# Row-projection order, an earlier key norm and four seven-product pairs in the last row unit of a two-layer decoder trunk

## Chip, cores and metric

The kernel runs on one core of one Trainium2 chip. The metric is the device time of one execution in microseconds (us), the median of three runs. A separate execution was profiled; every row below comes from it.

## The reference

Two layers, 256 tokens, model width 2048, all in float32. Each layer normalises the residual stream, multiplies it by one input projection `w_in` (2048 x 6160), runs two head groups side by side, multiplies their outputs by `w_o`, adds the residual, and does the same with a squared-ReLU MLP of width 8192.

```python
h = rms_norm(x, attn_norm)
g_q, g_k, g_v, g_gate, g_lr, s_q, s_k, s_v = split(h @ w_in)
o_gla = gated_linear_attention(g_q, g_k, g_v, log_sigmoid(g_lr @ w_gate_up + b_gate) / 16)
o_gla = rms_norm(o_gla, gla_out_norm) * silu(g_gate)
sq, sk = rms_norm(heads(s_q), sb_q_norm), rms_norm(heads(s_k), sb_k_norm)
o_sb = rms_norm(stick_breaking(sq, sk, s_v), sb_out_norm)
x = x + concat(o_gla, o_sb) @ w_o
x = x + square(relu(rms_norm(x, mlp_norm) @ w_up)) @ w_down
```

The stick-breaking group has 8 heads of 128; each head's queries and keys are normalised over those 128 elements before the scores.

## The kernel before

**Precision.** A float32 product is made of three matmuls: both operands are split into a high part (ScalarE, tile `whi` for weights, L868) and a low part (VectorE, tile `wlo`, L872: the value minus its high part), and high x high, high x low and low x high are added in PSUM (L967 to L969, 128 x 512 outputs).

**Units.** The large projections are cut into units of 1024 output columns. A unit works through eight pairs of contraction tiles (256 rows of weights each). A pair is done in one of three ways. A plain pair takes 8 products (two token halves x two column halves x two tiles), so 24 matmuls, in two steps. A fast pair uses a seven-product scheme for 2 x 2 blocks: 7 products, so 21 matmuls, in four steps of 2, 2, 2 and 1 products; VectorE first forms sums of weight blocks (tile `ts` and two overwritten quarters of `raw`, all L749) and then four low parts instead of two. An added pair is a plain pair whose low part is not made on VectorE: ScalarE writes the negated high part (`dlo`, L876) and a DMA issued by GpSimd adds the raw weights to it (L879).

**Order inside a unit.** It is a list of pair numbers written by hand; each time a pair number occurs, that pair's next step is issued. `STEPSI` with fast pairs `FASTI` serves the first row unit, `STEPSR` with `FASTR = (1, 3, 4, 5, 6)` the other three, `STEPS` with `FAST = (1, 3, 5, 6)` the MLP units. Pairs 2 and 7 are added pairs in all of these.

**Row units.** Ahead of each layer's attention four units of `w_in` are computed for the next layer in the order `ROWS = ("iv", "ik", "qk", "sq")`: values, keys of the stick-breaking heads, queries and keys of the linear attention, queries of the stick-breaking heads. Their results stay in SBUF as natural rows (`natural[kind, half]`), scaled by the row norm at L1106. For layer 0 the four units stand at 33.6 to 196.1 us of the profile, for layer 1 at 1066.2 to 1229.9 us. In `big_unit`, the first row unit of layer 1 also transposes the new residual (`turned`, L556) after its first and after its second step.

**Attention.** `attend` first opens a scratch region (`begin`, the list `opened["att"]`) whose memory belonged to the units until their last piece is done (`using["mlp"]`). Pieces made with `core` wait for that opening and are listed in `using["att"]`; pieces made with plain `add` do neither. `keys_queries(0)` names the keys first and then the queries of the first four heads; `turn_heads` calls `heads_norm`, which for each of two row blocks squares (ScalarE, L1348), sums per head (VectorE, L1351), then forms the reciprocal root (L459 to L468) and multiplies the rows by it (VectorE, L1330); then the heads are transposed (L1378) and copied with their scale (L1386) for the scores. Each square needs one of five `t2` buffers, held until its sum is made; at the opening in layer 0 two of the five are held by the constants and one by the small gains. Beside this, `narrow` runs the remaining projections of `w_in` on TensorE (L1243 to L1245) with the same high and low parts; the first of them, `va`, has 256 value columns and the 16 low-rank columns (128 x 272 outputs, weight parts 128 x 544).

**What sets the order.** A planner (`Plan`) simulates the engines with rough lengths. TensorE, SyncE and GpSimd issue most pieces in the order in which the program names them; VectorE and ScalarE take, of the pieces that are ready and find their buffers free, the one with the earliest due time; the attention's own TensorE pieces (`apart`) go ahead of the line when ready. The resulting order is fixed in the program. On the chip each engine runs its list strictly in that order and waits at semaphores.

Of the kernel before, what the change touches and what calls it, by code (L numbers as in the profile page):

```python
# [17 lines left out]
P = 128  # L18
# [5 lines left out]
FAST = (1, 3, 5, 6)  # L24
# [11 lines left out]
FIRSTR = 1  # L36
STEPSI = [0, 0, 1, 3, 1, 2, 2, 1, 1, 3, 4, 4, 5, 5, 5, 6, 5, 6, 6, 6, 7, 7]
FASTI = (1, 5, 6)
ADDEDI = ADDED
ROWS = ("iv", "ik", "qk", "sq")  # L40
BIG = ("up", "down") + ROWS
ACTS = 17
DEPTH = 2
# [182 lines left out]
def trunk_kernel(  # L226
# [556 lines left out]
    def unit_order(u):  # L783

        if u.kind == "o":
            return (STEPSO, STEPSP)[u.n2], (FASTO0, FASTO)[u.n2]
        if u.kind in ROWS[FIRSTR:]:
            return STEPSR, FASTR
        if u.kind == ROWS[0]:
            return STEPSI, FASTI  # L790
        return STEPS, FAST
# [359 lines left out]
    def big_unit(u, was, tail, after_tail):  # L1151
# [11 lines left out]
        for k, j in enumerate(order):  # L1163
# [21 lines left out]
            if k < 2 and was and was.kind == "o":  # L1185
                n = 2 * was.n2 + k
                for h2 in range(2):
                    done["up", 0, 2 * n + h2] = turned(
                        n, h2, ((5, 7), (1, 6))[k][h2], hm, "mlp", u.l, "sxh"
                    )  # L1190
            if 0 <= u.l < DEPTH - 1 and k < 2 and (u.at("down", 3, 1) or u.kind == "iv"):
                n = k + 2 * (u.kind == "iv")
                for h2 in range(2):
                    done["in", 0, 2 * n + h2] = turned(
                        n, h2, ((5, 7), (1, 6))[k][h2], hN, "attn", u.l + 1, "sxh"
                    )
# [118 lines left out]

    def inv_rms(ss, n, width, hold, *deps):

        box = {}

        def mean():  # L1320
            own = norm_tile("ny", hold, n), norm_tile("nt", hold, n)
            box["rr"], box["parts"] = inv_rms_parts(ss(), n, width, own)
            box["parts"][0]()

        a = core("DVE", 0.16, mean, *deps)
        b = core("ACT", 0.42, lambda: box["parts"][1](), a)
        return (lambda: box["rr"]), core("DVE", 0.72, lambda: box["parts"][2](), b)
# [8 lines left out]

    def heads_norm(rows, w, *deps):

# [21 lines left out]
        got[0].takes.append(slot_hold)  # L1360
        rr, ready = inv_rms(ss, len(rows) * nh, P, slot_hold, got)
        muls = [
# [146 lines left out]
    def normed(po, hold, o, *deps):  # L1509

        a = core("ACT", 0.6, lambda: nc.scalar.activation(o(), po(), AF.Copy), *deps)
        release(hold, a)
        return a, heads_norm([(o, a)], 512)

# [41 lines left out]
    def attend(l):  # L1556
# [78 lines left out]
        def turn_heads(key, nat, nat_hold, c, w, dst, h0, scale, deps, *more):  # L1635

            muls = heads_norm(rows(nat, c, w, deps), w, *more)
            for i in range(0, w // P, 2):
# [529 lines left out]
```

## Time and profile before

| | us |
|---|---|
| median of 3 runs (lowest, highest) | 2123.29 (2123.22, 2123.62) |
| the profiled execution | 2123.44 |
| its span, first to last instruction | 2121.7 |
| TensorE busy | 2110.9 (99%) |
| VectorE busy | 1969.7 (93%) |
| ScalarE busy | 1600.7 (75%) |
| GpSimd busy | 175.7 (8%) |

The span is 1.7 us shorter than the execution's time. The records of matmuls overlap: a 128 x 512 matmul is shown with 0.39 us, but the next one starts about 0.227 us later, and a 128 x 272 one starts about 0.12 us after the one before. So a gap on TensorE is read from the distance of two starts, less that pace; the profile's idle figure counts only what is left after the modelled end. The granted TensorE clock is 1.00 of 2.4 GHz throughout.

### The profile page before, as it was taken

Reading aid. Unit: us, or ns where it says so; the run is one execution under the profiler, and the core shown is the slowest. Engines: PE = TensorE matmul, PEld = TensorE weight load, DVE = VectorE, ACT = ScalarE, POOL = GpSimd, SP = SyncE. Lnnn points to the kernel's source line nnn. Section 1 sums busy time; section 2 is a strip of 40 time slices with the busy share of each in tenths; the row PEclk is TensorE's granted clock in tenths of the full one; section 3 lists DMA queues with packets and bytes.
Section 4 is the critical chain, followed back from the end, with each engine's and each line's share of the span. In section 5 each row is a group of like instructions: output and inputs, shape, how many; then the busy total and the mean of one; then the engine's idle time right before and its main releaser. Section 6 shows DMA issues by size and latency. Waiting matters only on the chain.

```text
span 2121.7 us, 28669 instructions
## 1 busy us (share of the span) xinstructions
PE 2110.9 (99%) x10043; PEld 1757.7 (83%) x10043; DVE 1969.7 (93%) x2672; ACT 1600.7 (75%) x2082; POOL 175.7 (8%) x234
## 2 busy tenths in 40 slices
PE   9999999999999999999999999999999999999999
PEld 7888888888888888888888888888888888888887
DVE  7998889999999999999999987899999999999998
ACT  8776878887678677677787776877876776776775
POOL 0111000000000000000010101000000000000000
PEclk9999999999999999999999999999999999999999
DMA  8887347888888888888888762778888888888886
GB/s 301 249 266 198 126 155 226 262 241 254 268 237 255 251 258 245 266 244 249 236 248 261 222 205 81 222 234 249 247 259 253 248 247 271 236 256 253 257 239 179
DMA packets 160724, 501.36 MB, mean 236 GB/s; under 512 B 14298, under 2 KB 23074, under 8 KB 160580
## 3 DMA queue, kind: packets, MB, share of 16 engines
q1 hardware_dynamic: 135236, 407.25, 55.5%
q0 software_dynamic: 25344, 92.29, 24.3%
q8 instruction: 79, 1.29, 0.2%
q14 instruction: 65, 0.53, 0.1%
HBM read 405.12 MB, written 2.10 MB: 192 GB/s over the span
## 4 chain that ended last, share of the span: by engine, by line
PE 97%; DVE 1%; ACT 1%; issue 0%; DMA 0%; DVEq 0%
DVE wlo L872 0%; ACT whi L868 0%; DVE xb L749 0%; PE m__462_2282 L1243 0%; PE m__12_144 L668 0%; PE m__468_2294 L1243 0%; PE m__2547_12117 L1243 0%; PE m__2549_12123 L1243 0%; DVE act L749 0%; PE m__579_2863 L1243 0%; PE m__579_2863 L1244 0%; PE m__468_2294 L1245 0%; PE m__462_2282 L1245 0%; PE m__2473_11750 L1245 0%; PE m__462_2282 L1244 0%
## 5 line engine op out<-in xcount | busy, mean ns | idle before, releaser
L868 ACT ACTIVATE whi<-raw 128x1024 fp32r<-128x1024 f32 (+2 forms) x944 | 901.8, 969 | 321.3 <-issue 48.8
L872 DVE TENSOR_TENSOR wlo<-raw,whi 128x1024 fp32r<-128x1024 f32 (+1 forms) x768 | 833.5, 1087 | 73.2 <-ACT whi L868 65.4
L879 POOL DMA_DIRECT2D dlo<-raw x176 | 149.9, 853 | 1758.3 <-ACT dlo L876 1129.9
L868 ACT ACTIVATE whi<-ts 128x1024 fp32r<-128x1024 f32 x176 | 186.5, 1060 | 83.9 <-DVE ts L749 3.3
L749 DVE TENSOR_TENSOR ts<-raw 128x1024 f32<-128x1024 f32 x176 | 214.9, 1221 | 3.4 <-DMA raw<-in_w_in_dram 0.8
L872 DVE TENSOR_TENSOR wlo<-ts,whi 128x1024 fp32r<-128x1024 f32 x176 | 214.5, 1219 | 1.9 <-ACT whi L868 1.7
L876 ACT ACTIVATE dlo<-raw 128x1024 fp32r<-128x1024 f32 x176 | 181.0, 1047 | 11.7 <-PE m__2009_9552 L968 1.7
L749 DVE TENSOR_TENSOR raw<-raw 128x512 f32<-128x512 f32 x176 | 120.9, 687 | 2.1
L749 DVE TENSOR_TENSOR raw<-ts,raw 128x512 f32<-128x512 f32 x176 | 120.5, 685 | 0.4
L1106 ACT ACTIVATE act<-act,st 128x512 f32<-128x512 f32 x96 | 66.2, 713 | 29.7 <-DVE act L749 29.2
L541 DVE TENSOR_TENSOR act<-t,act 128x512 fp32r<-128x512 f32 (+1 forms) x97 | 61.0, 635 | 0.0
L537 ACT ACTIVATE act<-t 128x512 fp32r<-128x512 f32 (+1 forms) x97 | 55.6, 585 | 0.2
L1351 DVE TENSOR_REDUCE st<-t 128x4 f32<-128x512 f32 x32 | 21.1, 680 | 7.1 <-ACT t L1348 7.1
L610 ACT ACTIVATE t<-xb 128x512 f32<-128x512 f32 x32 | 20.5, 655 | 9.3 <-DVE xb L749 8.9
L749 DVE TENSOR_TENSOR xb<-t,xb 128x512 f32<-128x512 f32 x40 | 27.3, 683 | 0.1
L541 DVE TENSOR_TENSOR sx<-t,sx 128x384 fp32r<-128x384 f32 (+1 forms) x44 | 23.6, 540 | 0.0
L537 ACT ACTIVATE sx<-t 128x384 fp32r<-128x384 f32 (+1 forms) x44 | 21.8, 500 | 0.6 <-DVE t L519 0.6
L519 DVE TENSOR_TENSOR t<-t,t 128x128 f32<-128x128 f32 x53 | 15.5, 292 | 1.8
L517 DVE TENSOR_TENSOR t<-t 128x128 f32<-128x128 f32 x53 | 15.4, 291 | 1.5
L1330 DVE TENSOR_TENSOR act<-act,st 128x512 f32<-128x512 f32 x24 | 15.5, 683 | 0.0
L516 DVE TENSOR_TENSOR t<-t 128x128 f32<-128x128 f32 x53 | 15.1, 285 | 0.0
L1348 ACT ACTIVATE t<-act 128x512 f32<-128x512 f32 x24 | 14.4, 620 | 0.1
(4359 smaller groups left out, 6121.2 us busy)
## 6 DMA issues: line engine op xcount, KB each, us to landing
raw<-in_w_up_dram SPq DMA_DIRECT2D x112, 1024.0 KB, 6.2
raw<-in_w_down_dram SPq DMA_DIRECT2D x112, 1024.0 KB, 6.6
dlo<-raw POOLq DMA_DIRECT2D x176, 512.0 KB, 6.4
raw<-in_w_in_dram SPq DMA_DIRECT2D x80, 1024.0 KB, 5.6
raw<-in_w_o_dram SPq DMA_DIRECT2D x30, 1024.0 KB, 8.5
raw<-in_w_up_dram SPq DMA_DIRECT2D x32, 512.0 KB, 5.7
raw<-in_w_down_dram SPq DMA_DIRECT2D x32, 512.0 KB, 5.9
raw<-in_w_in_dram SPq DMA_DIRECT2D x30, 512.0 KB, 5.3
```

The source lines that it names most:

```text
L519: nc.vector.tensor_tensor(e[0][:, 1, :], a12, e[0][:, 0, :], ALU.subtract)
L537: nc.scalar.activation(d[:, :, 0, :], src, AF.Copy)
L541: nc.vector.tensor_tensor(d[:, :, 1, :], src, f32(d[:, :, 0, :]), ALU.subtract)
L610: nc.scalar.activation(junk, xb[n][:, tt, :], AF.Square, accum_out=ssq[:, tt, n : n + 1])
L749: nc.vector.tensor_tensor(dst, a, b, op)
L868: nc.scalar.activation(view(box["h"]), src(), AF.Copy)
L872: nc.vector.tensor_tensor(view(box["l"]), src(), f32(view(box["h"])), ALU.subtract)
L876: nc.scalar.activation(box["l"], src(), AF.Copy, scale=-1.0)
L879: nc.gpsimd.dma_start(f32(box["l"]), src(), accum_op=ALU.add)
L1106: nc.scalar.activation(box[h][:, tt, :], box[h][:, tt, :], AF.Relu if into else AF.Copy, scale=norm["rr"][:, tt : tt + 1],)
L1330: nc.vector.tensor_tensor(dst.rearrange("p (h d) -> p h d", d=P), src.rearrange("p (h d) -> p h d", d=P), rr.unsqueeze(2).to_broadcast([P, ...
L1351: nc.vector.tensor_reduce(ss()[:, i * nh : (i + 1) * nh], sq()[:, :w].rearrange("p (h d) -> p h d", d=P), AX.X, ALU.add,)
```

## The change

Six edits. The linear attention's queries and keys become the second row unit and the stick-breaking keys the third. The last row unit gets a step list of its own with four fast pairs (1, 3, 5, 6); pair 4 becomes a plain pair there. The first row unit's list is reordered in two places (its second and third entries, with pair 2's second step two entries later, and its last entries). `heads_norm` and `inv_rms` take the function that makes their pieces as an argument, and for the keys of the first four heads (`SOON`) this is `add` instead of `core`. The literal `"iv"` becomes `ROWS[0]`.

```diff
-STEPSI = [0, 0, 1, 3, 1, 2, 2, 1, 1, 3, 4, 4, 5, 5, 5, 6, 5, 6, 6, 6, 7, 7]
+STEPSI = [0, 1, 0, 3, 1, 2, 1, 1, 2, 3, 4, 4, 5, 5, 5, 6, 5, 6, 6, 7, 6, 7]
 FASTI = (1, 5, 6)
 ADDEDI = ADDED
-ROWS = ("iv", "ik", "qk", "sq")
+SOON = (("k", 0),)
+LASTR = 3
+STEPSL = [0, 1, 1, 0, 1, 1, 3, 3, 2, 3, 2, 3, 4, 4, 5, 5, 6, 5, 5, 6, 6, 6, 7, 7]
+FASTL = FAST
+ROWS = ('iv', 'qk', 'ik', 'sq')
...
         if u.kind == "o":
             return (STEPSO, STEPSP)[u.n2], (FASTO0, FASTO)[u.n2]
+        if u.kind in ROWS[LASTR:]:
+            return STEPSL, FASTL
         if u.kind in ROWS[FIRSTR:]:
             return STEPSR, FASTR
...
-            if 0 <= u.l < DEPTH - 1 and k < 2 and (u.at("down", 3, 1) or u.kind == "iv"):
-                n = k + 2 * (u.kind == "iv")
+            if 0 <= u.l < DEPTH - 1 and k < 2 and (u.at("down", 3, 1) or u.kind == ROWS[0]):
+                n = k + 2 * (u.kind == ROWS[0])
...
-    def inv_rms(ss, n, width, hold, *deps):
+    def inv_rms(ss, n, width, hold, core, *deps):
...
-    def heads_norm(rows, w, *deps):
+    def heads_norm(core, rows, w, *deps):
...
-        rr, ready = inv_rms(ss, len(rows) * nh, P, slot_hold, got)
+        rr, ready = inv_rms(ss, len(rows) * nh, P, slot_hold, core, got)
...
-        return a, heads_norm([(o, a)], 512)
+        return a, heads_norm(core, [(o, a)], 512)
...
-            muls = heads_norm(rows(nat, c, w, deps), w, *more)
+            muls = heads_norm(add if key in SOON else core, rows(nat, c, w, deps), w, *more)
```

## Rows read from the trace of the kernel before

**Rows 1.** The page's first lines: span, and part 1, engines' busy time.

```profile
span 2121.7 us, 28669 instructions
PE 2110.9 (99%) x10043; PEld 1757.7 (83%) x10043; DVE 1969.7 (93%) x2672; ACT 1600.7 (75%) x2082; POOL 175.7 (8%) x234
```

**Rows 2.** Busy time by stretch, last row unit, both layers: length, PE, PEld, DVE, ACT, POOL.

```profile
155.98:196.10 40.12, 40.12 (x179) 33.22 (x177) 38.34 (x46) 29.58 (x35) 7.38 (x12) 1.00 0.78 208
...
1189.80:1229.92 40.12, 40.12 (x178) 33.22 (x177) 37.89 (x45) 29.27 (x35) 7.40 (x13) 1.00 0.76 203
```

**Rows 3.** Timeline, TensorE, layer 0's first narrow projection: start, length, instruction, [idle before <-releaser].

```profile
198.86 0.29 PE L1244 MATMUL m__372_1838<-wlo,act 128*128 128x272 f32 x1
198.98 0.28 PE L1245 MATMUL m__372_1838<-whi,act 128*128 128x272 f32 x1
200.00 0.39 PE L1243 MATMUL m__371_1833<-whi,act 128*128 128x272 f32 x1 [0.73 <-ACT whi L868]
200.88 0.39 PE L1244 MATMUL m__371_1833<-wlo,act 128*128 128x272 f32 x1 [0.49 <-DVE wlo L872]
```

**Rows 4.** Timeline, TensorE, the same place in layer 1.

```profile
1232.81 0.28 PE L1245 MATMUL m__2388_11323<-whi,act 128*128 128x272 f32 x1
1233.22 0.39 PE L1243 MATMUL m__2387_11319<-whi,act 128*128 128x272 f32 x1
1234.09 0.39 PE L1244 MATMUL m__2387_11319<-wlo,act 128*128 128x272 f32 x1 [0.48 <-DVE wlo L872]
```

**Rows 5.** Timeline, ScalarE, just after the last row unit of layer 0.

```profile
197.65 0.71 ACT L2002 ACTIVATE v<-act,st 128x512 f32<-128x512 f32 x1
198.26 1.14 ACT L1348 ACTIVATE t<-act 128x512 f32<-128x512 f32 x2
199.31 0.64 ACT L868 ACTIVATE whi<-raw 128x544 fp32r<-128x544 f32 x1
```

**Rows 6.** Timeline, VectorE, the same stretch.

```profile
198.91 1.28 DVE L1351 TENSOR_REDUCE st<-t 128x4 f32<-128x512 f32 x2 [1.52 <-ACT t L1348]
200.11 0.71 DVE L872 TENSOR_TENSOR wlo<-raw,whi 128x544 fp32r<-128x544 f32 x1
```

**Rows 7.** The load behind that weight part: SyncE's timeline, and the page's part 6.

```profile
189.24 0.37 SPq L1215 DMA_DIRECT2D raw<-in_w_in_dram  x1
raw<-in_w_in_dram SPq DMA_DIRECT2D x30, 512.0 KB, 5.3
```

**Rows 8.** Timeline, VectorE, a stretch of layer 0's last row unit.

```profile
168.38 1.22 DVE L749 TENSOR_TENSOR ts<-raw 128x1024 f32<-128x1024 f32 x1
169.51 1.22 DVE L872 TENSOR_TENSOR wlo<-raw,whi 128x1024 fp32r<-128x1024 f32 x1
170.65 0.69 DVE L749 TENSOR_TENSOR raw<-ts,raw 128x512 f32<-128x512 f32 x1
```

**Rows 9.** Timeline, VectorE, the rest of the key and query norms in layer 0.

```profile
202.56 0.29 DVE L459 TENSOR_SCALAR st<-st 128x8 f32<-128x8 f32 x2
203.43 0.16 DVE L466 TENSOR_TENSOR st<-st 128x8 f32<-128x8 f32 x1
207.50 1.29 DVE L1330 TENSOR_TENSOR act<-act,st 128x512 f32<-128x512 f32 x2
```

**Rows 10.** Timelines, TensorE, around the low-rank gate of layer 0.

```profile
212.00 0.38 PE L1681 MATMUL m__421_2074<-ident,lr 128*16 128x128 f32 x2
212.96 1.13 PE L1701 MATMUL m__425_2084<-lrT,wg 17*128 17x256 f32 x4 [0.57 <-DVE lrT L1687]
```

**Rows 11.** Timelines, VectorE and TensorE, layer 0's third row unit.

```profile
126.23 1.22 DVE L872 TENSOR_TENSOR wlo<-ts,whi 128x1024 fp32r<-128x1024 f32 x1
127.51 0.50 PE L968 MATMUL m__231_1180<-wlo,act 128*128 128x512 f32 x1 [0.40 <-DVE wlo L872]
```

**Rows 12.** Timelines, VectorE and TensorE, the start of layer 1's first row unit.

```profile
1069.61 0.69 DVE L749 TENSOR_TENSOR xb<-t,xb 128x512 f32<-128x512 f32 x1
1072.62 0.60 PE L556 MATMUL m__2090_9934<-ident,xb 128*128 128x128 f32 x4
```

## Prediction
> **What bounds the kernel.** The page's first part comes first: TensorE is busy for 99% of the span, VectorE for 93% [rows 1]. Next the busy time by stretch: the last row unit takes 40.12 us in both layers, without a gap, for the 177 matmuls of five fast and three plain or added pairs (5 x 21 + 3 x 24; the weight loads count 177), so 0.2267 us each, at a granted clock of 1.00, which is the 2.4 GHz level [rows 2]. TensorE's own count of matmuls therefore sets the length of nearly every stretch. VectorE is busy for 38.34 and 37.89 us of the same 40.12, so it has some 2 us to spare in that unit and no more [rows 2]. What is left are short waits, read from TensorE's timeline. Behind the last row unit of layer 0 the first narrow projection waits twice: starts that are 0.12 us apart just before are then 1.02 and 0.88 apart, so 1.66 us are lost [rows 3]; in layer 1 it is 0.41 and 0.87, 1.04 us [rows 4]. The first loss ends with a high weight part, the second with its low part. ScalarE's and VectorE's timelines tell why: both run their lists in order, and two squares of the head norm stand ahead of that high part, two sums ahead of that low part [rows 5, 6]. The data was not late: its load was issued at 189.24, and such loads land in about 5.3 us, well before 199.31 [rows 5, 7].
>
> **The change part by part.**
>
> *Pair 4 of the last row unit becomes plain.* It has 24 matmuls instead of 21, in two layers, so 6 more: 6 x 0.2267 = 1.36 us [rows 2]. All of it is on the path, since TensorE has no gap there. The Trainium skill ("TensorE: Matmul & The Clock Gate", section "Wait — 56ns, not 53.3ns?") has warm matmuls of 512 columns start N / 2.4 GHz plus 2.5 ns apart, 0.2157 us; the trace does not agree, and with that figure the six would be an estimated 1.29 us. I take the measured pace.
>
> *What pair 4 gives back on VectorE.* A fast pair costs it one wide sum (1.13 us to the next start), three wide low parts (1.14 each), two narrow sums and one narrow low part, 0.60 each by the distance of two starts in the pair of sums (1.28 less the last one's 0.68) [rows 6, 8]: 1.13 + 3.42 + 1.80 = 6.35. A plain pair has two wide low parts, 2.28. So 4.07 us of VectorE's time come free per layer. ScalarE makes two high parts instead of four. None of it is on the path by itself.
>
> *The keys' norm moves into that unit.* Two sums and two multiplications at 0.60, the small mean at about 0.12 (a pair shows 0.29) and three tiny steps of about 0.2: 3.1 us of VectorE [rows 6, 9], and two squares (1.14 for both) and two short activations on ScalarE [rows 5]. That is less than what pair 4 frees, so I cost it at nothing there; the cover is the 4.07 plus the 2 us of idle time. If the cover is gone, because the planner puts these pieces ahead of low parts that TensorE needs at once, the cost is up to 3.1 us per layer. It issues no DMA and passes none. The wait on the scratch's opening goes; what is late next is the queries' norm, whose projection ends only with that unit and whose pieces still wait for the opening.
>
> *The start of the attention, both layers.* With the keys' four ScalarE and eight VectorE pieces gone, the queries' two squares and two sums are first after the opening. Bounds: nothing is gained if both queries' squares and sums take exactly the keys' place, since the two free buffers that let the keys go first now let both queries go; all 1.66 and 1.04 us if the third weight part comes ahead of them. A loss is excluded here, as nothing is added ahead of that weight part. Between these I take the value of one sum, 0.60 us, which is the row nearest to the low part that ends the wait: pair 6's low parts, and with them the next load, should come earlier relative to TensorE, so the weight part should pass one of the two queries. So -0.6 us in each layer.
>
> *The low-rank gate of layer 0.* TensorE waits for `lrT`: the profile leaves it 0.57 us idle before the logits at 212.96 [rows 10], and the 0.16 by which a matmul's record runs over the next start (0.39 less 0.23 [rows 2, 3]) comes on top, 0.73 us. The head transposes and their copies move earlier by about the keys' share of VectorE's queue, which leaves ScalarE and TensorE free to start the next projection there. Bounds: 0 and 0.73; no row shows the new order, so I take about half, -0.4 us.
>
> *Keys third.* Second and third unit have the same shape and step list, the same eight loads on SyncE's queue and the same adds on GpSimd's; only the columns are exchanged, so nothing is passed. The one wait in the third unit of layer 0 (a low part ends at 127.45, its matmul starts at 127.51 after 0.40 idle, with the overlap 0.56 late) [rows 11] may stay, go, or come in the other unit: 0, between -0.6 and +0.6.
>
> *The first row unit's list.* The number of products is the same, so TensorE's work is. In layer 1 the second pair of transposes needs the last residual block, ready at 1070.30, and starts at 1072.62 [rows 12]. It now follows a step of two products instead of four, 1.36 us earlier, at about 1071.26: still 1.0 us after its data. Nothing; if that cover were gone, up to 1.36 us. The last entries only exchange a step of one product with half of pair 7; the adds land ahead of it. Nothing.
>
> **Sum:** 1.36 - 0.6 - 0.6 - 0.4 = -0.24 us against the profiled execution's 2123.44, so 2123.2; that execution stands 0.15 above the median of 2123.29, so 2123.0 as a median. With the page's figure for the matmul it would be 2122.98. A measurement of this kernel can tell about 0.2%, or 4.2 us, from no change, so the forecast is no change.
>
> **The rivals.**
>
> *The queries take the keys' place.* Both transition waits and the gate's stay as they are, and only the six matmuls show: 2123.29 + 1.36 = 2124.7. For it: the two buffers, and the fixed order of the lists. The same time comes out if the keys' norm is not placed early at all, because its due time is late and VectorE is hardly ever idle in that unit (the change would then not do what it says). Against it: 4 us come free on VectorE.
>
> *All waits go.* 1.36 - 1.66 - 1.04 - 0.73 - 0.56 = -2.63: 2120.7. For it: the load is there in time, and the freed VectorE time could put the third weight part ahead of all squares. Against it: the list is made from simulated landings, and one wait lies in a unit that is not changed in shape.
>
> *The keys' norm delays low parts in the last row unit.* Its place is VectorE's queue between the end of the third row unit and pair 4's steps, before the freed time arises. In the unit before, a low part that was 0.56 us late stopped TensorE at once [rows 11], so 0.60 us pieces can do the same. Price: at worst both layers in full, 2 x 3.1 + 1.36 = 7.6: 2130.9. It decides the sign once more than 2.9 of the 6.2 us are uncovered. Against it: the pieces have late due times, so they go in only when nothing more urgent is ready.
>
> **How the numbers follow.** The forecast has a chance of 0.50, the queries in the keys' place 0.28, all waits gone 0.16; these three lie within 4.2 us. The delayed low parts have 0.04. The last 0.02 is for an order of the attention that saves over 4.2 us, which no row shows. That makes faster 0.02, same 0.94, slower 0.04. The range goes from all waits gone, 2120.7, to the queries' rival with a new wait of the third unit's size beside it, 2124.7 + 0.6 = 2125.3; the last rival and what lies past these ends are left out.
>
> **What would show it.** In the changed profile: the last row unit should be 40.8 us long with 180 weight loads; squares and sums of the key norm should lie inside it, ahead of the opening, and VectorE should be busy for about 1 us less there, 37 us. After the opening only two squares should remain, and the distances of starts at the first narrow projection should sum to less: a low part directly behind one sum means 0.6 saved, behind two means the first rival. A gap on TensorE in the last row unit that ends with a low part, with a sum or a multiplication of the norm ahead of it, would mean the third rival. Any gap at the second transposes of layer 1's first row unit would show that cover gone. The prediction is wrong if the attention stretches themselves, not the transitions, change by more than 1 us.

## The result and the profile after

The changed kernel takes 2125.98 us in the median of 22 runs (2125.55 to 2127.68), the kernel before 2123.27 in as many beside it: a ratio of 1.0013, interval [1.0007, 1.0019]. That is 2.7 us slower: small, but the interval excludes no change, and the median lies above the forecast's range. Of 30 runs (eight were added later) six lie at 2127.0 to 2127.7 and the others at 2126.4 or below; a second profile further on shows what the upper group does. The profiled execution took 2125.61 us with a span of 2123.9.

The page's first lines (they answer to [rows 1]), and busy time by stretch for the two last row units (columns as in [rows 2]):

```profile
span 2123.9 us, 28655 instructions
PE 2114.4 (100%) x10049; PEld 1759.8 (83%) x10049; DVE 1961.2 (92%) x2662; ACT 1597.4 (75%) x2078; POOL 172.5 (8%) x234
```

```profile
156.44:197.26 40.82, 40.82 (x182) 33.78 (x180) 37.46 (x49) 28.42 (x36) 8.71 (x16) 1.00 0.77 209
1189.87:1230.67 40.80, 40.80 (x181) 33.78 (x180) 36.04 (x47) 28.25 (x37) 7.61 (x13) 1.00 0.70 194
```

TensorE is as busy as ever, and has 3 matmuls more in each of these units. VectorE's busy time fell by 0.9 and 1.9 us there, where about 1 was expected; in layer 1 one low part of 0.7 us for the next projection moved out of the unit as well. So the total hides the story, and TensorE's timeline was cut into stretches by its own starts, in both traces (us):

| stretch | before | after | difference |
|---|---|---|---|
| start to the first row unit, layer 0 | 33.56 | 33.93 | +0.37 |
| first row unit, layer 0 | 41.48 | 42.27 | +0.79 |
| second and third, layer 0 | 80.94 | 80.24 | -0.70 |
| last row unit, layer 0 | 40.12 | 40.82 | +0.70 |
| attention, layer 0 | 112.42 | 111.61 | -0.81 |
| o units and feed-forward, layer 0 | 757.72 | 757.45 | -0.27 |
| first three row units, layer 1 | 123.57 | 123.55 | -0.02 |
| last row unit, layer 1 | 40.12 | 40.80 | +0.68 |
| attention, layer 1 | 131.08 | 131.71 | +0.63 |
| o units and feed-forward, layer 1, to the last matmul | 756.37 | 757.19 | +0.82 |

They sum to +2.19, and the last matmul starts 2.20 later. Two of the largest terms are in places that the prediction costed at nothing or did not mention. One is the first row unit. TensorE's timeline there, then SyncE's and GpSimd's issues and the time to landing of the two added transfers, after:

```profile
44.81 0.39 PE L973 MATMUL m__66_415<-whi,act 128*128 128x512 f32 x1
45.69 0.50 PE L974 MATMUL m__66_415<-dlo,act 128*128 128x512 f32 x1 [0.49 <-DMA dlo<-raw]
```

```profile
36.40 1.02 POOL L885 DMA_DIRECT2D dlo<-raw  x1 [35.01 <-ACT dlo L882]
...
36.86 0.37 SPq L846 DMA_DIRECT2D raw<-in_w_in_dram  x1
...
DMA to landing us min/median/max: 9.2/9.7/10.2
```

and the same three in the kernel before:

```profile
34.63 0.37 SPq L840 DMA_DIRECT2D raw<-in_w_in_dram  x1
...
36.95 1.92 POOL L879 DMA_DIRECT2D dlo<-raw  x2 [35.57 <-ACT dlo L876]
...
DMA to landing us min/median/max: 5.5/6.2/7.0
```

Before, the 1 MB load leaves 2.3 us ahead of the adds, and the first add lands in 5.5 us. After, the load leaves between the two adds, the first takes 9.2 us, and TensorE starts 0.88 us after its previous start instead of 0.23. What let the load go is a low part of VectorE, 0.03 and 0.02 us ahead of it (VectorE's timeline, before, then after):

```profile
33.38 1.22 DVE L872 TENSOR_TENSOR wlo<-raw,whi 128x1024 fp32r<-128x1024 f32 x1
```

```profile
35.62 1.22 DVE L878 TENSOR_TENSOR wlo<-raw,whi 128x1024 fp32r<-128x1024 f32 x1
```

It is the second low part of this list before and the third after, which fits pair 0's second product standing one place later; the rows do not name the buffer. The other place is the first o unit of layer 1:

```profile
1367.82 0.39 PE L973 MATMUL m__2658_12725<-whi,act 128*128 128x512 f32 x1
1368.72 0.50 PE L974 MATMUL m__2658_12725<-dlo,act 128*128 128x512 f32 x1 [0.51 <-DMA dlo<-raw]
```

```profile
1359.36 0.37 SPq L846 DMA_DIRECT2D raw<-in_w_o_dram  x1
...
DMA to landing us min/median/max: 9.1/9.1/9.1
```

The same picture: a load leaves at 1359.36, the add at 1359.54, it takes 9.1 us, and TensorE loses 0.67. Before, the add leaves at 1356.48, the load only at 1357.96, and the add lands in 5.28 (GpSimd's two adds and their times to landing, then the load):

```profile
L879 POOL DMA_DIRECT2D dlo<-raw x2: 854/860/866, 1356.5 to 1358.4; - x2
DMA to landing us min/median/max: 5.3/7.6/10.0
...
1357.96 0.37 SPq L840 DMA_DIRECT2D raw<-in_w_o_dram  x1
```

It also leaves earlier against its unit, 4.5 us ahead of the unit's first matmul instead of 2.8.

At the places that the prediction did speak of: the first narrow projection of layer 0 (answers to [rows 3]) and of layer 1 ([rows 4]).

```profile
200.27 0.29 PE L1249 MATMUL m__371_1841<-whi,act 128*128 128x272 f32 x1
200.88 0.39 PE L1250 MATMUL m__371_1841<-wlo,act 128*128 128x272 f32 x1 [0.33 <-DVE wlo L878]
...
1230.67 0.28 PE L1249 MATMUL m__2381_11316<-whi,act 128*128 128x272 f32 x1
1230.99 0.39 PE L1250 MATMUL m__2381_11316<-wlo,act 128*128 128x272 f32 x1
```

Of 1.66 us lost in layer 0, 0.49 are left, of 1.04 in layer 1, 0.20. VectorE's timeline in the last row unit of layer 0 holds the keys' norm, two sums and two multiplications among the low parts:

```profile
166.16 0.67 DVE L1357 TENSOR_REDUCE st<-t 128x4 f32<-128x512 f32 x1
...
169.62 0.68 DVE L1357 TENSOR_REDUCE st<-t 128x4 f32<-128x512 f32 x1
...
178.62 0.69 DVE L1336 TENSOR_TENSOR act<-act,st 128x512 f32<-128x512 f32 x1
...
182.10 0.78 DVE L1336 TENSOR_TENSOR act<-act,st 128x512 f32<-128x512 f32 x1
```

The wait for `lrT` [rows 10] is gone as well. In its place TensorE now waits a little later, for a wide low part behind a wide high part (TensorE, then VectorE, then ScalarE):

```profile
213.67 0.36 PE L1249 MATMUL m__423_2088<-whi,act 128*128 128x256 f32 x1
214.83 0.39 PE L1250 MATMUL m__423_2088<-wlo,act 128*128 128x256 f32 x1 [0.79 <-DVE wlo L878]
...
213.55 1.23 DVE L878 TENSOR_TENSOR wlo<-raw,whi 128x1024 fp32r<-128x1024 f32 x1 [1.11 <-ACT whi L874]
...
212.09 0.47 ACT L1614 ACTIVATE v<-m__371_1841,st 128x256 f32<-128x256 f32 x1
212.47 1.05 ACT L874 ACTIVATE whi<-raw 128x1024 fp32r<-128x1024 f32 x1
```

VectorE was idle; the low part could not begin before ScalarE's high part, which stands behind three copies and a scaling in ScalarE's list. That costs 1.04 us (1.16 less 0.12). In layer 1 a smaller one of this kind is new, the scores behind a copy:

```profile
1242.25 0.70 PE L1409 MATMUL m__2418_11494<-act,act 128*128 128x256 f32 x2 [0.34 <-ACT act L1392]
```

### The profile page after: what moved, and what is told of

Its sections match the earlier page's. It is cut to its first block, busy times and chain, and to the rows that moved or that the text cites. A ratio compares the mean times of both kernels' runs of the same rounds, so it can differ in the third digit from the quotient of the medians.

```text
span 2123.9 us, 28655 instructions
## 1 busy us (share of the span) xinstructions
PE 2114.4 (100%) x10049; PEld 1759.8 (83%) x10049; DVE 1961.2 (92%) x2662; ACT 1597.4 (75%) x2078; POOL 172.5 (8%) x234
## 3 DMA queue, kind: packets, MB, share of 16 engines
q8 instruction: 79, 1.29, 0.2%
## 4 chain that ended last, share of the span: by engine, by line
PE 96%; DMA 1%; DVE 1%; ACT 1%; issue 0%; ACTq 0%; DVEq 0%
DMA dlo<-raw 1%; DMA raw<-in_w_in_dram 0%; DVE wlo L878 0%; DVE xb L753 0%; PE m__460_2289 L1249 0%; PE m__459_2282 L1249 0%; PE m__2536_12098 L1249 0%; ACT whi L874 0%; PE m__2534_12092 L1249 0%; ACT act L570 0%; PE m__2462_11738 L1249 0%; PE m__2461_11730 L1249 0%; PE m__574_2854 L1249 0%; PE m__574_2854 L1250 0%; PE m__459_2282 L1251 0%
## 5 line engine op out<-in xcount | busy, mean ns | idle before, releaser
L878 DVE TENSOR_TENSOR wlo<-raw,whi 128x1024 fp32r<-128x1024 f32 (+2 forms) x766 | 831.5, 1087 | 83.7 <-ACT whi L874 74.3
```

Of the source, the lines that this page charges most:

```text
L878: nc.vector.tensor_tensor(view(box["l"]), src(), f32(view(box["h"])), ALU.subtract)
```

## The experiments

The theory after the two traces: the six matmuls cost what was said, the waits at the attention's start go, and what makes the kernel slower are added low parts that land late because a load leaves beside them, once by the first row unit's list, once by the attention's new end in layer 1. The rivals: the norm's new place, the last row unit's list, the new order, or one execution's chance. All runs beside the kernel before, medians, with the stretches that moved (us; "o" is o units and feed-forward). The stretches are those of one profiled execution. The intervals reach about 0.0009 to either side, 1.9 us, so a difference of under 2 us between two medians is not clear of noise by itself; such prices are read from the stretches.

| run | median (before) | ratio, interval | first unit, L0 | last unit, L0 / L1 | attention, L0 / L1 | o, L0 / L1 |
|---|---|---|---|---|---|---|
| first_list_undone | 2125.19 (2123.51) | 1.0008 [1.0, 1.0017] | 41.48 | 40.83 / 40.80 | 111.60 / 131.71 | 757.48 / 757.07 |
| norm_undone | 2127.06 (2123.51) | 1.0018 [1.0009, 1.0026] | 42.23 | 40.80 / 40.80 | 111.87 / 131.82 | 759.05 / 756.62 |
| last_list_undone | 2126.88 (2123.51) | 1.0016 [1.0007, 1.0025] | 42.45 | 40.87 / 40.67 | 111.44 / 132.00 | 759.37 / 756.31 |
| order_undone | 2130.05 (2123.51) | 1.003 [1.0019, 1.0042] | 42.29 | 40.80 / 40.80 | 112.02 / 130.13 | 761.07 / 757.29 |
| first_list_alone | 2124.14 (2123.39) | 1.0003 [0.9994, 1.0012] | 41.48 | 40.12 / 40.12 | 112.43 / 131.08 | 757.69 / 756.37 |
| order_alone | 2123.35 (2123.39) | 1.0 [0.9991, 1.0009] | 41.48 | 40.12 / 40.12 | 112.43 / 131.08 | 757.62 / 756.36 |
| norm_alone | 2128.31 (2123.39) | 1.0023 [1.0014, 1.0032] | 41.48 | 40.40 / 40.47 | 112.54 / 131.73 | 759.34 / 756.33 |
| last_list_alone | 2126.54 (2123.39) | 1.0016 [1.0007, 1.0025] | 41.48 | 40.80 / 40.80 | 111.91 / 131.85 | 759.33 / 756.81 |
| start_kept | 2129.05 (2123.57) | 1.0026 [1.0016, 1.0036] | 41.48 | 40.80 / 40.80 | 112.01 / 131.70 | 759.25 / 757.33 |
| o_add_off | 2128.24 (2123.57) | 1.002 [1.0012, 1.0029] | 41.48 | 40.82 / 40.80 | 114.32 / 131.73 | 759.12 / 756.35 |
| layer0_only | 2123.36 (2123.57) | 0.9999 [0.999, 1.0008] | 41.48 | 40.85 / 40.12 | 111.59 / 131.08 | 757.54 / 756.37 |
| layer1_only | 2124.70 (2123.58) | 1.0005 [0.9996, 1.0014] | 41.48 | 40.12 / 40.80 | 112.41 / 131.71 | 757.71 / 756.33 |

**The first row unit's list, undone and alone.**

```
 first_list_undone (changed kernel):   -STEPSI = [0, 1, 0, 3, 1, 2, 1, 1, 2, ...]   +the old list
 first_list_alone (kernel before):     -STEPSI = [0, 0, 1, 3, 1, 2, 2, 1, 1, ...]   +the new list
```

> The changed kernel with the old list of the first row unit. Theory (collision): the new list takes pair 0's second product later, so its buffer comes free later, the next load of a weight block starts beside the two adds of pair 2's low part, and the adds land 3 us later than before; TensorE then waits 0.76 us in the first row unit of layer 0. With the old list the adds land in under 7.5 us again, that wait is gone, the unit takes 41.5 us instead of 42.27, and the time is 2126.0 - 0.8 = 2125.2. Rival (start-up or the new order of units delays the adds, not the list): the add still lands in over 9 us, the unit stays at 42.3 us and the time at 2126.0. The waits behind layer 1's attention stay as they are by either, so the o unit and feed-forward of layer 1 stay near 757.2 us.

> The kernel before with the new list of the first row unit alone. Theory (the list makes pair 0's buffer late, and the next load runs beside pair 2's adds): the first row unit of layer 0 is 42.3 us long instead of 41.48, pair 2's first add takes over 9 us to land, nothing else moves: 2123.4 + 0.8 = 2124.2. Rival (the collision needs the other parts too): the unit stays at 41.5 us and the time at 2123.4.

Undone, the first add lands in 5.4 us and the unit takes 41.48, 0.79 less; the median falls by 0.8 as it stands, by 1.0 against its own runs of the kernel before. Alone, the median rises by 0.75, as the theory has it, but the interval includes no change, and the profiled execution shows no wait: it took 2123.06 us, the lowest of its 11 runs. Its time to landing and TensorE's timeline:

```profile
DMA to landing us min/median/max: 8.4/9.1/9.8
```

```profile
44.78 0.39 PE L973 MATMUL m__66_415<-whi,act 128*128 128x512 f32 x1
45.01 0.39 PE L974 MATMUL m__66_415<-dlo,act 128*128 128x512 f32 x1
```

The add took 8.44 us here and landed at 44.67, 0.34 ahead of its matmul. In o_add_off, which has the new list as well, it took 8.53 and was in time too (unit 41.48). In the other six traces with this list it took 9.0 to 9.3 and came late, by 0.6 to 0.8 us. So the list makes the add slow in all eight; whether TensorE waits hangs on the last half microsecond.

**Only the start of the list.**

```
-STEPSI = [0, 1, 0, 3, 1, 2, 1, 1, 2, 3, ...]
+STEPSI = [0, 0, 1, 3, 1, 2, 1, 1, 2, 3, ...]
```

> The changed kernel, where the list of the first row unit begins with pair 0's two products together, as before, and keeps its other new entries. Theory (pair 0's second product, put behind pair 1's first, makes its buffer late, so that the load runs beside pair 2's adds): the first add lands in under 7.5 us, the first row unit of layer 0 is 41.5 us long, 2126.0 - 0.8 = 2125.2. Rival (it is the later entries, pair 2's second product or the last four, that move the adds or the load): the add still takes over 8.4 us, the unit stays at 42.3 and the time at 2126.0.

In the unit the theory holds: with pair 0's two products together the load leaves 2.0 us ahead of the add, which lands in 5.7, and the unit takes 41.48. The time does not hold at all: 2129.05. In layer 0's attention TensorE now loses 1.8 us to a low part, and then 2.4 us to an added part in the o unit. The profiled execution took 2127.40, the lowest of the nine and the only one with a mean granted clock of 1.000 (the others 0.999), so part of the median goes with the clock, of which more below. An edit of the first unit's list had changed the order of an attention 260 us later. Across the traces the first add of the first row unit is sorted by one number, when the nearest load leaves against it:

| run | load less add, us | add lands in, us |
|---|---|---|
| before | -2.32 | 5.48 |
| start_kept | -1.97 | 5.67 |
| order_alone | -1.63 | 5.98 |
| before_again | -1.39 | 6.21 |
| layer0_only | -1.28 | 6.59 |
| after_again | +0.34 | 8.98 |
| after | +0.46 | 9.25 |
| o_add_off | +0.57 | 8.53 |
| first_list_alone | +0.60 | 8.44 |

**The keys' norm and the last row unit's list.**

```
 norm_undone (changed kernel):        -SOON = (("k", 0),)   +SOON = ()
 last_list_undone (changed kernel):   -LASTR = 3            +LASTR = 4
 norm_alone:        the kernel before with SOON = (("k", 0),)
 last_list_alone:   the kernel before with LASTR = 3
```

> The changed kernel with the keys' norm at its old place, behind the opening of the attention's scratch. Theory (the norm's new place rearranges the attention and makes layer 1's end later, so that the o unit's added low part lands late): attention of layer 1 goes from 131.7 back to about 131.1 us, the o unit and feed-forward from 757.2 to 756.4, and the attention of layer 0 goes back from 111.6 to 112.4: 2126.0 - 0.6 - 0.8 + 0.8 = 2125.4. Rival (the last row unit's list does that, by way of its loads and buffers): layer 1 keeps its 1.4 us and layer 0 loses its gain: 2126.8.

> The changed kernel with the last row unit on the list of the other row units, five fast pairs, so 6 matmuls less. Theory (the six matmuls are the cost, the freed VectorE time buys little): both last row units go from 40.8 to 40.1 us, the rest stays: 2126.0 - 1.4 = 2124.6. Rival (pair 4's 4 us of VectorE are what lets the norm in): the key norm's 3 us of pieces now stand ahead of low parts, TensorE stops inside the last row unit or just behind it by 1 to 3 us a layer, and the time is 2126.6 to 2130.

> The kernel before with the keys' norm begun ahead of the opening, the last row unit on its old list and the old order (so the norm belongs to the third unit's projection with the queries third, and to the last but one here). Theory (without pair 4's VectorE time the norm's pieces delay low parts and the next projection's weight): a stop of 0.2 to 0.8 us inside each last row unit and a wait behind it of 2.0 us instead of 1.66 in layer 0, and 1.3 instead of 1.04 in layer 1: 2123.4 + 2.1 = 2125.5. Rival (the stops of the run without the last list came from the order of the units): no stop in the last row unit and a time of 2123.4, within 0.5.

> The kernel before with the new list of the last row unit alone. Theory (the list alone brings what is gained behind the unit, the norm's place adds little): six matmuls cost 1.4 us, and the waits at the first narrow projection, 1.66 and 1.04, go: 2123.4 + 1.4 - 2.7 = 2122.1. Rival (the norm must go early too): the waits stay, 2123.4 + 1.4 = 2124.8. Third reading (an earlier or later end of the attention brings the o unit's added low part against a load): 1 to 2 us more in the o unit of one layer than either of the two says.

Either of the two taken out of the changed kernel makes it later, but only by 0.8 us (norm_undone) and 0.7 (last_list_undone) against its own runs of the kernel before, which is within the intervals. With the norm and no pair 4 freed (last_list_undone), TensorE stops inside the last row unit and longer than ever behind it:

```profile
189.64 0.39 PE L973 MATMUL m__312_1542<-whi,act 128*128 128x512 f32 x1
190.09 0.50 PE L974 MATMUL m__312_1542<-wlo,act 128*128 128x512 f32 x1
...
200.36 0.28 PE L1251 MATMUL m__377_1855<-whi,act 128*128 128x272 f32 x1
201.99 0.39 PE L1249 MATMUL m__376_1849<-whi,act 128*128 128x272 f32 x1 [1.34 <-ACT whi L874]
202.75 0.39 PE L1250 MATMUL m__376_1849<-wlo,act 128*128 128x272 f32 x1 [0.37 <-DVE wlo L878]
```

2.14 us are lost at the projection where it was 1.66, so pair 4's VectorE time does pay for the norm. Its rival was right there, the theory's 2124.6 was not. With the list and no early norm (last_list_alone, norm_undone) nothing is left of the transition's waits in either layer, so the list ends them without the norm's new place. Yet 2122.1 does not come out for last_list_alone: the third reading does, by 2.1 us in layer 0's o unit. With the norm alone the stops inside the units are there too, more of them than its theory had (41.14 us in the third and 40.40 in the last unit of layer 0, 40.88 and 40.47 in layer 1), but the transition's wait of layer 0 stays at 1.65; that of layer 1 goes. And all four kernels lose 1.3 to 1.7 us in layer 0's o units and feed-forward, three of them at a matmul that takes an added part (1.9 to 2.5 us), last_list_undone with 0.8 us there and 1.6 at transposes behind it. Neither of the theories for norm_undone (2125.4, 2126.8) had it. What differs there is when the added part leaves: 2.0 us ahead of the unit in norm_undone and last_list_alone, 1.45 us behind its start in last_list_undone and norm_alone (at 311.07, the unit begins at 309.62); in the kernel before at 304.40, 4.1 us ahead. It takes 9.5 and 9.8 us in the first two, which would have been in time before (9.85 in first_list_alone, 4.1 us ahead), and only 4.9 and 6.6 in the others.

**The order of the units.**

```
 order_undone (changed kernel):  -ROWS = ('iv', 'qk', 'ik', 'sq')   +ROWS = ("iv", "ik", "qk", "sq")
 order_alone: the kernel before with ROWS = ('iv', 'qk', 'ik', 'sq')
```

> The changed kernel with queries ahead of keys again in the order of the units (so the keys are third again, ik before qk). Theory (the order cost nothing and brought the third unit's 0.7 us): the third unit of layer 0 is 40.8 us long again instead of 40.1, and the time is 2126.0 + 0.7 = 2126.7. Rival (the new order is what puts layer 1's attention late, since the norm that goes early is another part's): layer 1's attention and the o unit give back 1.4 us, 2126.0 + 0.7 - 1.4 = 2125.3. Under a third reading, that the wait in the third unit belongs to the plan as a whole and not to the order, the unit stays at 40.1 us and the time at 2126.0.

> The kernel before with the keys' projection third and nothing else. Theory (the wait in the third unit belongs to the order): that unit of layer 0 is 40.1 us long instead of 40.82, the rest stays: 2123.4 - 0.7 = 2122.7. Rival (the order also changes layer 1's attention, which was 130.1 us long with the order undone and 131.7 with it): the 0.7 goes, but the attention of layer 1 is 131.7 instead of 131.1: 2123.3. Third reading: the order alone makes the o unit's added low part late, as in three of the four runs so far; then the o unit and feed-forward of one layer are 1 to 3 us longer.

Alone, the order changes nothing that a median shows (2123.35 against 2123.39). Undone, the third unit's stop is there, in both layers (40.88 and 40.87 us), and layer 1's attention gives back 1.6 us, so theory and rival are both right at their place; but the whole costs 4 us more. Over all traces the third unit of layer 0 is longer than 40.2 us in five of seven with the old order (40.29 to 41.14, the longest with the norm in that unit) and in none of twelve with the new one (40.12 to 40.20). So the order seems to end that stop, though no median shows it. A low part is 1.8 us late in layer 0's attention, then comes the longest stop of all at an added part, and with it something new. TensorE's timeline, and the granted clock by stretch (length, PE busy, clock, DMA share, GB/s):

```profile
315.86 0.39 PE L973 MATMUL m__623_3109<-whi,act 128*128 128x512 f32 x1
318.69 0.50 PE L974 MATMUL m__623_3109<-dlo,act 128*128 128x512 f32 x1 [2.44 <-DMA dlo<-raw]
```

```profile
315.80:318.70 2.90, 0.46 (x3) 1.00 1.07 212
318.70:319.60 0.90, 0.90 (x4) 1.00 1.07 214
319.60:323.00 3.40, 3.40 (x10) 0.53 0.14 27
```

Behind 2.6 us of stop the clock goes to about half, the 1.2 GHz level, for 3.4 us, and eight matmuls start 0.43 instead of 0.23 apart: another 1.6 us. All six runs of this kernel have a mean granted clock of 0.999.

**The added part of the o unit, taken off the transfers.**

```
-return j in (ADDEDO if u.kind == "o" else ...
+return j in ((ADDEDO if u.n2 else ADDEDO[1:]) if u.kind == "o" else ...
```

> The changed kernel with pair 5's low part made by VectorE instead of by an added transfer in the first o unit of each layer. Theory (in layer 1 TensorE waits 0.9 us for that transfer because it is issued 2.8 us ahead of the unit and takes 9.1 us beside loads): the wait goes, the o unit and feed-forward of layer 1 take 756.4 us instead of 757.2, those of layer 0, where the transfer was in time, stay at 757.4: 2126.0 - 0.8 = 2125.2. Rival (VectorE is what is short there, and the adds only hide it): two more low parts of 1.14 us end a wait of 1 us or more in both layers, 2126.0 or later.

In layer 1 the theory holds to the number, 756.35. In layer 0 the rival does: a low part in the attention is 1.8 us late, and the part now made by VectorE is late in its turn, by 1.0 us. The 114.32 us of the attention in this trace also hold a fall of the granted clock (0.50 at 217 to 218 us, 0.62 at 218 to 221) behind the stop of 1.04 us at the wide low part.

```profile
316.66 0.49 PE L973 MATMUL m__622_3107<-whi,act 128*128 128x512 f32 x1
317.92 0.50 PE L974 MATMUL m__622_3107<-wlo,act 128*128 128x512 f32 x1 [0.77 <-DVE wlo L878]
```

**Adds that fall due earlier.**

```
-LAND, ADD = 7.0, 6.0
+LAND, ADD = 7.0, 8.5
```

> The changed kernel, planned with a landing of the added low parts that is 2.5 us longer (8.5 instead of 6.0 behind GpSimd's part), so that they fall due earlier. Theory (layer 1's o unit loses 0.8 us since the add is issued too late for a landing of 9.1 us): it is issued 4 us or more ahead of the unit, the wait goes, the o unit and feed-forward of layer 1 take 756.4 us; the first row unit stays at 42.3, since there the negation already follows the load's landing at once: 2126.0 - 0.8 = 2125.2. Rival (the new dates only move the loads, and the wait comes back elsewhere): a wait of 0.7 us or more for an added low part in some o unit, 2126.0 or later.

> The same with the old list of the first row unit. Theory (the two losses are separate and add up): first row unit 41.5 us and o unit with feed-forward of layer 1 756.4 us: 2126.0 - 0.8 - 0.8 = 2124.4. Rival (as for the run before): 2125.2 or later, with an added low part late in an o unit.

> The kernel before with the same longer landing, as a control. Theory (no added low part is late there): nothing to gain, 2123.4 within 0.4, all stretches as before. Rival (any new plan of the attention's end costs, whatever it is for): 2124.4 or later, by a low part of VectorE late in the attention or by an added one in the o unit of layer 0.

These took 2133.56, 2133.32 and 2129.75 us (before 2123.94), ratios 1.0048 [1.0034, 1.0062], 1.0044 [1.0032, 1.0057] and 1.0026 [1.0016, 1.0036]. The theory fell. In layer 1 no added part is late any more, yet the o units and feed-forward take 758.17, 757.59 and 757.23 us and not 756.4, with new waits of 0.5 to 0.7 us for low parts of VectorE. In layer 0 the add now leaves 0.9 us ahead of its unit (2.0 in the control) instead of 4.4 and 4.1, and TensorE stops for 2.4 us there, in the kernel before too (1.8). So a new date for the adds costs in the kernel before as well, where no added part was late.

**Layer by layer.**

```
 both: the changed kernel with the old first list, and
 layer0_only:  +if u.kind in ROWS[LASTR:] and u.l < 0:     +add if key in SOON and not l else core
 layer1_only:  +if u.kind in ROWS[LASTR:] and u.l >= 0:    +add if key in SOON and l else core
```

> The changed kernel with the old list of the first row unit, and the last row unit's list and the keys' early norm only ahead of layer 0's attention; layer 1 has both as before. Theory (the parts gain in layer 0 and lose in layer 1, each at its place): layer 0 as in the run with the old first list, 0.4 us better than before in the last row unit, the attention and the o unit together, layer 1 as before (40.1, 131.1 and 756.4 us): 2123.4 - 0.4 = 2123.0, or 2122.3 if the third unit's stop of 0.7 us is there in every execution of the kernel before. Rival (the o unit's added low part of layer 1 is late again, since loads are placed anew): 757 us or more there, 2123.6 to 2124.2.

> The changed kernel with the old list of the first row unit, and the last row unit's list and the keys' early norm only ahead of layer 1's attention; layer 0 has both as before. Theory (each layer's gain and loss are its own): layer 0 as before (last row unit 40.1 us, attention 112.4, o unit and feed-forward 757.7), layer 1 as in the changed kernel (40.8, 131.7, 757.1): 0.7 + 0.6 + 0.7 more than before, 2123.5 + 2.0 = 2125.5. Rival (layer 1's loss comes from what layer 0's attention does to the loads ahead): layer 1 stays near 40.8, 131.1 and 756.4, 2124.2. Third reading (any new plan can put a transfer late): an added low part late in layer 0's o unit, 2125.5 or later with layer 1 as in either.

Ahead of layer 0 alone the parts gain 0.28 us by the stretches (+0.73 in the last row unit, -0.83 in the attention, -0.18 behind it), and the whole is the same as before. Ahead of layer 1 alone they lose 1.3 us by the stretches and 1.1 by the medians (the interval includes no change): the matmuls (+0.68) and the attention (+0.63) as in the changed kernel, but not the o unit. There the add is issued at 1359.43, at nearly the time of the changed kernel, and the load only at 1360.32:

```profile
1360.32 0.37 SPq L846 DMA_DIRECT2D raw<-in_w_o_dram  x1
...
DMA to landing us min/median/max: 5.7/8.1/10.5
```

The first of the two adds lands in 5.7 us, ahead of its use. It leaves 2.84 us ahead of the unit, as in the changed kernel. So the o unit's 0.8 us is not the attention's later end by itself; it takes the slow landing too, and what differs is the load beside the add. No run moved that load alone.

**Both kernels once more.**

> The kernel before once more, unchanged, for a second execution with a profile. Theory (the stop of 0.56 us in the third row unit of layer 0 and the 0.3 us earlier start belong to the first execution alone, since the same program with another first list ran that unit in 40.12): the third unit is 40.1 us long, and TensorE begins the first row unit at 33.9 to 34.3 instead of 33.56. Rival (the stop belongs to the program): 40.8 us again.

> The changed kernel once more, unchanged. Theory (its waits are of the program): TensorE waits again at the first row unit's added part of layer 0 (0.76 us), at the scores in layer 1's attention (0.50) and at the o unit's added part of layer 1 (0.9), each within 0.2 us, and the third unit is 40.12 us long. Rival (they hang on how an execution's transfers fall): one of them is under 0.3 us, or there is a new one of over 0.5.

The kernel before showed its third unit's stop again, at half its size (40.51 us; [rows 11] had 0.56):

```profile
127.52 0.39 PE L967 MATMUL m__231_1180<-whi,act 128*128 128x512 f32 x1
128.00 0.50 PE L968 MATMUL m__231_1180<-wlo,act 128*128 128x512 f32 x1
```

and TensorE began the first row unit at 34.36, not 33.56. Both vary between executions of one program, so the +0.37 of the table cannot be put down to the change, and of the -0.70 only as much as a given execution of the kernel before happens to lose. In the changed kernel all three waits came again (0.75, 0.50 and 0.64 us). The rival was half right as well: this execution took 2127.3 us, and its attention in layer 0 was 1.5 us longer with no new stop. The same 3 us, in the first and the second execution:

```profile
217.80:220.80 3.00, 3.00 (x27) 1.00 0.96 313
```

```profile
217.80:220.80 3.00, 3.00 (x16) 0.50 0.89 277
```

The granted clock is 1.00 (2.4 GHz) in one and 0.50 (1.2 GHz) in the other, behind the same stop of 1.04 us at the wide low part. That is the upper group of the runs: all six have a mean granted clock of 0.999, the other 24 and every run of the kernel before whose clock is on record have 1.000.

## Why the prediction was wrong

Its failing step is "the adds land ahead of it. Nothing.", on the first row unit's list. That was argued from the order of the last entries and of pair 7's adds; the entry that mattered is the second one, and the add that came late is pair 2's. Pair 0's second product behind pair 1's first makes pair 0's buffer come free later (the load that waits for it left at 36.86 instead of 34.63), and so the next load leaves beside the adds. The transposes' cover, which the prediction did check, held. Its price is 0.79 us in the unit, from before to after and from after back to undone; the medians of undone and alone, 0.8 to 1.0 and 0.75 us, agree with it, but neither is clear of noise by itself. That this edit slows the add is shown by start_kept, where only the second entry's place is taken back.

The second failure is an omission: the list of what a moved step drags along stopped at the attention. The o unit's added part leaves 1.7 us later against its unit, takes 9.1 us to land when a load leaves beside it, and TensorE loses 0.67 at that matmul, 0.82 us in the stretch; o_add_off and layer1_only each remove it, in two different ways.

The third failure is the largest against the sum, 1.23 us: the -0.6 forecast for the start of the attention in layer 1. The wait there did go, by 0.84, but the stretch came out 0.63 longer, so the rest of that attention lost 1.47 us; the sum had no term for it.

Point by point otherwise. The six matmuls: 1.36 expected, 0.70 and 0.68 measured, right, at the trace's pace. The estimate from the Trainium skill's pace, 1.29 ("TensorE: Matmul & The Clock Gate", section "Wait — 56ns, not 53.3ns?"), is 0.09 under the measured 1.38; the trace does not agree with that pace. The keys' norm: right that it lies in the last row unit at no cost and that pair 4's time is the cover; last_list_undone shows the price without it. VectorE's busy time there, 37 us expected, was 37.46 and 36.04. The first narrow projection: -0.6 expected in each layer, -1.17 and -0.84 measured; the share that goes was too small, since the third weight part came ahead of all squares and not behind one. Of the two reasons that the prediction gave, the keys' norm gone from there and pair 6's low parts being earlier, it is the last row unit's list that counts in layer 0: the waits go with the list alone (norm_undone, last_list_alone), and with the norm alone 1.65 stays. The `lrT` wait: -0.4 expected, all of 0.73 went, but the prediction did not ask what TensorE would meet next, and that was the low part behind ScalarE's copies, +1.04. Together, -1.17 - 0.73 + 1.04 = -0.86, these are nearly all of the -0.81 of layer 0's attention; that it lies near the forecast's -1.0 is luck, since the new wait was not foreseen. In layer 1, 0.50 of the 1.47 lost is the scores' wait; no other gap there is as long, and no run separates the rest. Either part alone, norm or list, brings the 0.6 to 0.9 there. Keys third: the third unit's wait went, one of the outcomes that were left open; its size varies from execution to execution of the kernel before, and the median shows nothing.

By the medians of the runs that separate the places: first list +0.75, layer 0 -0.2, layer 1 +1.1, and by the stretches the o unit's wait of 0.8, which came with neither layer alone: 2.45 of the 2.7. No single one of the three medians is clear of noise, so the sum is a consistent account and not a measurement.

The falsifier that was named, attention stretches that change by more than 1 us without their transitions, did trip in layer 1: without the waits at the first narrow projection, -0.81 and +0.63 become +0.36 and +1.47. No change by the bound of 0.2% is what came (0.13%), but the range excluded the time: its upper end was the six matmuls with all waits kept and one new wait of 0.6 us, and here two new waits of a transfer came, beside two new ones in the attention, in a kernel whose added parts take 5 to 10 us to land. What remains open is why the plan of layer 0's attention takes one of two ends. In ten of the 15 edited kernels an added part is late in the o unit behind it (in o_add_off the part of VectorE in its place), in the other five and in both originals not, and no single edit separates the groups. Two numbers do: in the good group the first add leaves 4.1 to 4.4 us ahead of the unit's first matmul, in the nine others that have such an add from 2.0 us ahead to 1.45 behind; and in eight of the ten a low part of VectorE comes 1.3 to 2.2 us late near the end of that attention (296 to 306 us), in the good group none. What makes the plan so is not shown.

## What to carry to other kernels

When a step in an ordered list moves, follow the buffer that it frees to the load that waits for it, and then look at what else is on the DMA queues when that load leaves: the price was in a transfer of another pair, 9 us on. A term of an edit that re-makes the whole plan needs a bound for new waits on transfers anywhere downstream, not only where the edit is; here such waits were 0.4 to 2.6 us. Repeat the profile of a kernel before reading stops of half a microsecond as its own.

## What the runs showed of the hardware

In the first row unit and in layer 1's first o unit, the first of the two added transfers of 512 KB by GpSimd lands in 4.9 to 5.8 us when the nearest 1 MB load left 1.9 us and more ahead or 0.9 us and more behind it, in 6.0 to 6.6 when it left 1.3 to 1.8 ahead, and in 8.4 to 9.4 when it left from 0.2 us ahead to 0.6 behind. The second of the two is slower, 7.0 to 10.6 us, and does not follow this. In layer 0's o unit the order is less clean: with the load 0.9 to 1.1 us ahead it takes 6.8 to 9.9. GpSimd's instruction itself lasts 0.85 to 1.0 us, so a load that leaves while it runs seems to go ahead of the add; that is a reading of the table, and no run varied it alone.

A stop of TensorE need not end with its length. Behind stops of 1.04 us (after_again), 2.4 us (adds_early) and 2.6 us (order_undone) the granted clock fell to about 0.5, the 1.2 GHz level, for some 3 us, which cost 1.5 us more in the first and 1.6 in the last; behind the same 1.04 us in another execution, and behind stops of 1.8 to 2.5 us in five others (start_kept, norm_undone, norm_alone, last_list_alone, before_adds_early), it stayed at 1.00. What decides it no run shows.
